# Stick-breaking attention: products of two heads side by side, the causal mask moved onto the exponentials

## The chip, the core and the metric

The kernel runs as one program on one core of a Trainium2 chip. The metric is the device time of one execution in microseconds (us). The engines of the core are TensorE (PE in the rows: matrix products; PEld: its weight loads), VectorE (DVE), ScalarE (ACT), GpSimd (POOL) and SyncE (SP), which issues the transfers. SBUF is the working memory. PSUM is the memory that the products are written to: eight banks of 512 float32 for each of 128 partitions.

## The reference, cut to what matters

The reference is a small network of two blocks on 256 tokens of 1024 features: an attention block with two kinds of heads ("diff" and "moba"), a mixture of 32 experts, a Mamba layer, a gated embedding, a stick-breaking attention and a second gated embedding. The change touches the stick-breaking attention above all, which has 16 heads of 64 features:

```python
for blk in range(s // SB_BLOCK):                      # two blocks of 128 queries
    q0 = blk * SB_BLOCK
    kend = q0 + SB_BLOCK
    z = jnp.einsum('bhtd,bhsd->bhts', q[:, :, q0:kend], k[:, :, :kend])
    strict = s_idx < t_idx
    log_keep = jnp.where(strict, jax.nn.log_sigmoid(-z), 0.0)
    suffix = lax.cumsum(log_keep, axis=3, reverse=True) - log_keep
    weights = jnp.where(strict, jnp.exp(jax.nn.log_sigmoid(z) + suffix), 0.0)
    outs.append(jnp.einsum('bhts,bhsd->bhtd', weights, v[:, :, :kend]))
return (o * jax.nn.silu(gate)) @ w_out
```

Only keys before the query count (`strict`). A head has 128 x 128 scores in its first block of queries and 128 x 256 in its second, 384 columns side by side.

## The kernel before

The program is written with a framework that orders each engine's instructions when it compiles, by the order in which they are emitted and by when it expects their inputs; each engine then works through its own list in order. A tile of a pool is handed on to its next user when all readers of the old one are done, and a pool of `bufs=2` has two such tiles. `mm` puts a product behind the earlier ones into the same PSUM tile.

The eight PSUM banks are: three for the dense products (`dn`), two single ones for the scores (`at`, taken with `ps_at`), two for transposes (`tp`) and one for attention outputs (`pv`).

Dense products split each weight into two parts (`wh` by ScalarE or VectorE, L172 and L176; `wl` by VectorE, L183, or, for some, GpSimd, L187). `nat` yields after each three of its products; `kchunk`, `qchunk` and `vchunk` make the keys, queries and values of eight heads each. `merge` emits two generators side by side, each at the pace of its number of steps. The stick-breaking part is emitted as `stick(0)`, the first eight heads, beside 42 steps (`CUT`) of dense work, and then `stick(1)`, the last eight, beside the other 22; the queries and keys of the last eight heads are made in the first of the two.

`stick_first` makes the weights of one head. Three accumulating products into one bank: a mask of 0 and -1e30 by an identity (`mneg_r`, `ident_r`), then queries times keys for the two blocks of queries, on the lower or upper 64 rows of the array as the head is even or odd. ScalarE takes Abs, Exp and Ln (L1396), which gives ln(1 + exp(-|z|)). VectorE makes max(z, 0) + that (`sp`, L1411) and min(z, 0) - that (`w`, L1413), runs a cumulative sum of `sp` from the right (L1415, restarted at the ends of the blocks by the zeros of `scm`), and subtracts (L1416); ScalarE takes Exp. Two heads later (`LAG`) `stick` transposes the weights (L1432), copies them (L1434) and, for every second head, multiplies two heads with their values (L1442), gates the result and splits it into two parts (L1446 to L1448).

In the first block, `products` (L509) takes two tiles from `ps_at` and issues the score products of two heads in turn, one on the lower and one on the upper half of the array's rows. Its heads run on VectorE in `softmax` (L518).

Of the kernel before, what the change touches and what calls it, by code (L numbers as in the profile page):

```python
# [20 lines left out]
P = 128  # L21
# [7 lines left out]
# columns of the small-parameter pack  # L29
# [9 lines left out]
# columns of the constant packs  # L39
# [25 lines left out]
def merge(*parts):  # L65
    """Runs generators side by side, each at the pace of its number of steps."""
    live = [[g, n, 0] for g, n in parts]
    while live:
        live.sort(key=lambda a: a[2] / a[1])
        a = live[0]  # L70
        a[2] += 1
        try:
            next(a[0])
        except StopIteration:
            live.remove(a)
# [13 lines left out]
class Ring:  # L89
    """Weight tiles of 1 MB in the order of use, loaded ahead into the free slots of a few pools."""  # L90
# [6 lines left out]
    def add(self, name, pool, slots, bufs=None, once=False):  # L97
        """Slots of a tag of a pool, for use again and again or once."""
        self.pools[name] = (pool, bufs or slots, once)
        self.free[name] = self.free.get(name, 0) + slots  # L100
        self.fill()
# [21 lines left out]
    def issue(self):  # L123
        """All reads of the oldest tile taken are in the program."""
# [7 lines left out]
class Halves:  # L132
    """Two tiles [128, 4, 2, 256] as one of [128, 8, 2, 256]."""
# [11 lines left out]
class Dense:  # L145
    """Splits weight tiles into two parts of twelve bits each, ahead of their products."""
# [55 lines left out]
def tile_network(ctx, tc, A, out, dbg=None):  # L202
# [14 lines left out]
    def mm(o, lhsT, rhs, **kw):  # L217
        """A product, issued behind the earlier ones into the same bank."""
# [15 lines left out]

    def ps_at():
        return ps("at", 2, banks[0])
# [14 lines left out]
    # ---------------------------------------------------------------- loads that come first  # L251
# [47 lines left out]
    def keep_warm(n, behind, bank=None):  # L299
        """Products that nobody reads: the tensor engine's clock stays up while it waits for data."""  # L300
# [8 lines left out]
    # ---------------------------------------------------------------- helpers  # L309
    def rsqrt(ss, n, inv):  # L310
        """1 / sqrt(ss * inv + eps) on [128, n]."""
# [6 lines left out]
    def row_scale(tok, junk, behind):  # L318
        """1 / root mean square of each token."""
# [6 lines left out]
    def feed(t, c, outs, src=None):  # L326
        """Half c of the columns of x transposed, times gains: outs are (gain, tile [128, 8, 2, 256] for two parts).

        The products of both token tiles come when the second is there."""
# [31 lines left out]
    def scale_of(t, r, sums, eps=EPS):  # L361
        """1 / root of the sum of the two halves' squares."""
# [8 lines left out]
    def tick():  # L371
        """Half a weight tile has been multiplied: emits what was put off until now."""
# [6 lines left out]
    def nat(dense, xT, groups, evac, bank=ps_dn, by_token=False):  # L379
        """out[token, 512 columns] += xT^T w, weights moving; groups: units (chunk, first block of rows) of a chunk.  # L380

        By token: a unit's two halves for one token tile, then for the other."""
# [28 lines left out]
    def trans(dense, xT, evac):  # L411
        """out[512 columns, token], K = 1024, weights standing; evac gets two blocks of 128 columns."""
# [22 lines left out]
    def head_norm(p, acc, rtok, gain, dst, tok, kb, back=False):  # L435
        """acc [128 tokens, 8 heads x 64] -> root mean square per head, transposed, times the gain.

        acc still lacks the factor rtok of its token."""
# [24 lines left out]
    # ================================================================ first block: attention  # L463
# [45 lines left out]
    def products(q, k, blk, both):  # L509
        """The products of two heads, side by side in the upper and the lower half of the array."""  # L510
        pas = [ps_at() for _ in both]
# [6 lines left out]
    def softmax(pa, b):  # L518
        """Exponentials of the masked scores of one head less their maximum, and 1 / their sums."""
# [16 lines left out]
    def transposed(w):  # L536
        """[128 queries, 384] -> [128 keys, 384]: keys 0.. for all queries, keys 128.. for the later ones."""
# [21 lines left out]
    def forward(b, acc):  # L559
        """The parts of block b of yT, and acc with its queries in their order."""  # L560
# [73 lines left out]
    # bias of a distance, as a Hankel table through DRAM: queries run backwards within their tiles of 128  # L634
    dramp = phA.enter_context(tc.tile_pool(name="dramA", bufs=1, space=DRAM))
    pl = ps_at()
# [13 lines left out]
    # -lambda on all partitions  # L650
# [42 lines left out]
    def turn(t, c):  # L693
        """Half c of the columns of x transposed: after the second token tile."""
# [31 lines left out]
    # ================================================================ router  # L726
# [3 lines left out]
    phP.close()  # L730
    phP = ExitStack()
# [17 lines left out]
    # the first group that has the largest logit  # L749
# [16 lines left out]
    # rank of an expert in its group: the larger logits, and the equal ones before it  # L766
# [14 lines left out]
    # assignments over the 32 experts, and their number up to each token  # L781
# [9 lines left out]
    # place of a token among its expert's slots, from 1 on; 0 where it isn't the expert's  # L791
# [3 lines left out]
    def dispatch(g):  # L795
        """One-hot of the slots of four experts."""
# [6 lines left out]
    # more tokens than slots at any expert?  # L803
# [7 lines left out]
    # weights of the two experts  # L811
# [27 lines left out]
    # ---------------------------------------------------------------- tokens beyond the slots  # L839
# [55 lines left out]
    # ---------------------------------------------------------------- experts, four at a time  # L895
    def combine_T(g):
        """Slot against token for the four experts of g: one-hot, and the weight of each slot."""
# [12 lines left out]
    def gather(g, j, xg):  # L910
        """Transposed inputs of the slots of four experts, four blocks of 128; they lack the factor of their token."""
# [18 lines left out]
    def slot_scale(g):  # L930
        """The factor of each slot's token."""
# [16 lines left out]
    def ple_proj(i):  # L948
        """Half of the embedding's projection."""
# [14 lines left out]
    def in_turn(i):  # L964
        """A product behind the earlier one of the experts: the weights come in this order."""
# [5 lines left out]
    def warm(g, j):  # L971
        """Between the products of the last experts."""
# [3 lines left out]
    def next_xg(g):  # L976
        """The inputs of the four experts after those of g."""
# [75 lines left out]
    phP.close()  # L1053
    phP = ExitStack()
# [3 lines left out]
    # ================================================================ second block: Mamba layer  # L1058
# [29 lines left out]
    def time_steps():  # L1088
        """Time steps, their running sums times A, on [32 heads, 256 tokens]."""
# [4 lines left out]
        pdt = ps_at()  # L1094
# [9 lines left out]
        # ln(1 + e): the logarithm of the rounded sum, and what the rounding took  # L1104
# [26 lines left out]
    # halves: silu(v) = (v/2) (1 + tanh(v/2))  # L1131
# [28 lines left out]
    def gate_z(dst):  # L1160
        """Twice silu."""
# [14 lines left out]
    def ssd(g):  # L1176
        """The state-space heads of group g, gated, with the gain: yTg[g]; rg[g]: 1 / root mean square."""
        pa = ps_at()
# [50 lines left out]
        def sum_up():  # L1229
# [3 lines left out]
            # the squares carry the factor 4 of twice silu  # L1233
# [40 lines left out]
    # ================================================================ gated embedding of a layer  # L1274
    def ple(i, up, sums, then):
        """up holds x times the gain, sums four times the mean squares."""
# [20 lines left out]
        # the last columns one token tile after the other, the end of them in small pieces  # L1297
# [29 lines left out]
    scm = dw_.tile([P, W386], F, name="scm")  # L1327
    nc.sync.dma_start(scm, A["scm"])
    ident_r = dw_.tile([P, P], R, name="ident_r")
    nc.vector.tensor_copy(ident_r, ident)  # L1330
    mneg_r = dw_.tile([P, W386], R, name="mneg_r")
    nc.vector.tensor_copy(mneg_r, mneg)
    sums_k = new_sums()

    def to_stick(tok, c):
# [272 lines left out]
```

## Time and profile before

| what | value |
|---|---|
| time, median of 3 runs | 777.23 us |
| the three runs | 777.46, 773.49, 777.23 us |
| span of the profiled execution, first to last instruction | 773.4 us |
| granted TensorE clock, mean over the span | 0.991 of full speed |
| busy, share of the span: PE, PEld, DVE, ACT, POOL | 95%, 67%, 60%, 49%, 14% |
| stick-breaking part | about 650.5 to 735.5 us of the span |

The profile belongs to one execution, whose span is the time from its first to its last instruction; its own time is not listed apart from the three runs, of which the fastest lies 0.1 us above that span and the median 3.8 us. Busy time is an average over stages with different limits; the stage between 650.5 and 735.5 us is the one to look at here.

### The profile page before, as it was taken

How to read it: one execution, taken by the hardware profiler on the slowest of the kernel's cores; microseconds unless marked ns; L12 is line 12 of the kernel's file. 1: busy time of each engine (PE TensorE's matmuls, PEld its weight loads, DVE VectorE, ACT ScalarE, POOL GpSimd, SP SyncE). 2: the span in 40 equal slices, each digit the busy share in tenths (PEclk: the TensorE clock that was granted, in tenths of full speed). 3: DMA queues.
4: the chain of work that ended last, by engine and by line, in shares of the span. 5: the costliest groups of instructions: out<-in, count | busy, mean ns of one | idle time of the engine just before them, and what ended most of it. 6: DMA issues, size and time to landing. Idle time of an engine off the chain costs nothing. (4 is left out here: it accounts for less than half of the span.)

```text
span 773.4 us, 11374 instructions
## 1 busy us (share of the span) xinstructions
PE 734.3 (95%) x4386; PEld 517.3 (67%) x4386; DVE 467.0 (60%) x887; ACT 380.1 (49%) x712; POOL 110.2 (14%) x74
## 2 busy tenths in 40 slices
PE   8999999997899998899999989999899999999997
PEld 5777767542534334333999988897688897766686
DVE  5658675411101102104999979899888656888974
ACT  6557654210121111103776848475577645756763
POOL 0302300000000000000022231413300301242100
PEclk9999999999899999999999999999999999999999
DMA  8994767899999999983466445444354455222211
GB/s 334 423 404 147 264 238 264 308 412 422 413 422 418 421 420 420 422 369 108 165 242 227 160 151 194 175 164 163 110 184 163 164 177 205 72 104 100 107 56 55
DMA packets 29878, 188.77 MB, mean 244 GB/s; under 512 B 3215, under 2 KB 5852, under 8 KB 8188
## 3 DMA queue, kind: packets, MB, share of 16 engines
q1 hardware_dynamic: 29164, 186.70, 62.5%
q8 instruction: 36, 0.59, 0.3%
q10 hardware_dynamic: 416, 0.62, 0.3%
q0 software_dynamic: 240, 0.67, 0.2%
q14 instruction: 22, 0.18, 0.1%
HBM read 186.88 MB, written 1.10 MB: 243 GB/s over the span
## 5 line engine op out<-in xcount | busy, mean ns | idle before, releaser
L183 DVE TENSOR_TENSOR wl<-w,wh 128x1024 fp32r<-128x1024 f32 x116 | 150.4, 1301 | 49.8 <-ACT wh L172 49.6
L172 ACT ACTIVATE wh<-w 128x1024 fp32r<-128x1024 f32 x117 | 123.1, 1057 | 100.2 <-PE dn L219 86.0
L219 PE MATMUL dn<-uC,wh 128*128 128x256 f32 x640 | 119.5, 288 | 0.6 <-ACT uC L346 0.3
L219 PEld LDWEIGHTS dn<-uC,wh 128*128 128x128 f32 x640 | 100.5, 193 | 2.5 <-issue 1.6
L219 PE MATMUL dn<-uC,wl 128*128 128x256 f32 x320 | 91.2, 285 | 0.0
L187 POOL TENSOR_TENSOR wl<-w,wh 128x1024 fp32r<-128x1024 f32 x18 | 46.6, 2587 | 146.2 <-DVE wh L176 98.4
L997 PE MATMUL pv<-w,xg 128*32 128x512 f32 x512 | 65.8, 596 | 0.0
L219 PEld LDWEIGHTS dn<-uC,wl 128*128 128x128 f32 x320 | 61.9, 193 | 0.2 <-issue 0.2
L315 POOL TENSOR_TENSOR rs_r<-rs_v,mhalf 128x8 f32<-128x8 f32 (+2 forms) x26 | 42.7, 1643 | 119.7 <-DVE rs_v L313 103.5
L928 DVE TENSOR_SCALAR xg<-gx,idg 128x128 f32<-128x128 f32 x30 | 10.5, 350 | 72.0 <-PE gx L219 54.0
L219 PEld LDWEIGHTS gx<-disp,x 128*128 128x128 f32 x240 | 31.1, 200 | 23.6 <-issue 15.3
L219 PE MATMUL dn<-wh,uk 128*128 128x512 f32 x128 | 44.5, 406 | 0.0
L219 PE MATMUL dn<-wh,yTg 128*128 128x512 f32 x128 | 44.2, 407 | 0.3
L219 PE MATMUL gx<-disp,x 128*128 128x128 f32 x240 | 36.2, 296 | 7.7 <-PEq L845 5.0
L936 DVE COPY rs<-tp 128x1 f32<-128x1 f32 x8 | 1.3, 159 | 68.2 <-PE tp L219 68.2
L997 PEld LDWEIGHTS pv<-w,xg 128*32 128x32 f32 x512 | 16.1, 109 | 37.6 <-issue 34.4
L1021 PE MATMUL tp<-w,hT 128*32 128x512 f32 x256 | 37.3, 627 | 1.3 <-DVE hT L1015 1.3
L219 PE MATMUL acc<-oe,cmb 128*128 128x512 f32 x64 | 31.4, 613 | 6.4 <-ACT oe L1027 6.3
L219 PE MATMUL dn<-wh,u 128*128 128x512 f32 x104 | 36.4, 405 | 0.6 <-ACT wh L172 0.6
L926 ACT ACTIVATE xg<-gx,idg 128x128 f32<-128x128 f32 x30 | 11.0, 367 | 52.4 <-DVE xg L928 52.4
L1005 ACT ACTIVATE sl<-pv,rs 128x256 f32<-128x256 f32 x8 | 3.8, 473 | 65.7 <-PE pv L997 37.8
L1027 ACT ACTIVATE oe<-tp,sw 128x512 f32<-128x512 f32 x16 | 11.0, 686 | 43.9 <-PE tp L1021 43.9
(430 smaller groups left out, 1529.0 us busy)
## 6 DMA issues: line engine op xcount, KB each, us to landing
w<-in_wm SPq DMA_DIRECT2D x96, 1024.0 KB, 14.0
w<-in_m SPq DMA_DIRECT2D x28, 1024.0 KB, 4.7
w<-in_ks SPq DMA_DIRECT2D x16, 1024.0 KB, 4.7
w<-in_wi SPq DMA_DIRECT2D x11, 1024.0 KB, 14.3
w<-in_pg SPq DMA_DIRECT2D x8, 1024.0 KB, 4.7
w<-in_wo SPq DMA_DIRECT2D x4, 1024.0 KB, 15.7
eb<-adram SPq DMA_DIRECT2D x8, 512.0 KB, 4.9
w<-in_so SPq DMA_DIRECT2D x4, 1024.0 KB, 4.8
```

The lines of the kernel that those rows point to most:

```text
L172: i = nc.scalar.activation(whf, w, AF.Copy)
L183: i = nc.vector.tensor_tensor(wl.rearrange("p a b -> p (a b)"), w, whf.bitcast(F), op=OP.subtract)
L187: nc.gpsimd.tensor_tensor(wl.rearrange("p a b -> p (a b)"), w, whf.bitcast(F), op=OP.subtract)
L219: i = nc.tensor.matmul(o, lhsT, rhs, **kw)
L315: nc.gpsimd.tensor_tensor(r, v, mhalf.to_broadcast([P, n]), op=OP.pow)
L926: nc.scalar.activation(xg[:, k, :], pg_[:, b * P:(b + 1) * P], AF.Copy, scale=gain_of(5, k))
L928: nc.vector.tensor_scalar(xg[:, k, :], pg_[:, b * P:(b + 1) * P], gain_of(5, k), None, op0=OP.mult)
L936: nc.vector.tensor_copy(rs, pt[:, 0:1])
L997: in_turn(nc.tensor.matmul(pgu[32 * e:32 * e + 32, :], xg[:, k, 32 * e:32 * e + 32], w[:, e * 512:(e + 1) * 512], start=k == 0, stop=k == ...
L1005: nc.scalar.activation(sl, pgu[:, 0:256], AF.Silu, scale=rs)
L1021: in_turn(nc.tensor.matmul(po[32 * e:32 * e + 32, :], hT[:, k, 32 * e:32 * e + 32], w[:, e * 512:(e + 1) * 512], start=k == 0, stop=k == 1 ...
L1027: nc.scalar.activation(oe, po, AF.Copy, scale=sw)
```

## The change

The scores get one tile of two adjacent banks in place of two single banks (`ps_pair`, `bufs=1`); where one bank is wanted, `ps_at` gives out the two halves of such a tile in turn, or a whole pair is taken and half of it used. The first attention's `products` write into such a pair too.

In the stick-breaking part `stick_products` issues the score products of two heads in turn, as `products` does, each pair of heads into one pair of banks. The mask product, its identity and its rounded copy are gone. The scores are now unmasked: `valid` (1 where a key counts) and `anew` (0 where the cumulative sum starts again, at each query's last valid key) are made once, by five small VectorE instructions. Since the sum starts with the key's own term, one subtraction of it from z gives the logarithm of the weight, so the second of the two VectorE instructions on z (L1413) is gone, and z is read by the subtraction instead. After the exponential, GpSimd multiplies the two 128-column triangles of each head by `valid`. The order in `stick` is by pairs: products and weights of a pair, then transposes, copies and value products of the pair before. The value products go through `mm`, too.

```diff
+    halves_at = []
+
+    def ps_pair():
+
+        halves_at.clear()
+        return banks[0].tile([P, 2, 512], F, name="at", tag="at", bufs=1)
+
     def ps_at():
-        return ps("at", 2, banks[0])
+
+        if not halves_at:
+            t = ps_pair()
+            halves_at.extend((t[:, 1, :], t[:, 0, :]))
+        return halves_at.pop()
...
     def products(q, k, blk, both):
-        pas = [ps_at() for _ in both]
+        pair = ps_pair()
+        pas = [pair[:, i, :] for i in both]
...
-    pl = ps_at()
+    pl = ps_pair()[:, 0, :]
...
-        pdt = ps_at()
+        pdt = ps_pair()[:, 0, :]
...
-        pa = ps_at()
+        pa = ps_pair()[:, 0, :]
...
-    scm = dw_.tile([P, W386], F, name="scm")
-    nc.sync.dma_start(scm, A["scm"])
-    ident_r = dw_.tile([P, P], R, name="ident_r")
-    nc.vector.tensor_copy(ident_r, ident)
-    mneg_r = dw_.tile([P, W386], R, name="mneg_r")
-    nc.vector.tensor_copy(mneg_r, mneg)
+    ones_s = dw_.tile([P, W386], F, name="ones_s", tag="pth", bufs=2)
+    nc.sync.dma_start(ones_s, A["scm"])
+
+    valid = dw_.tile([P, W386], F, name="valid")
+    nc.vector.tensor_scalar(valid, mneg, 0.0, None, op0=OP.is_equal)
+    anew = dw_.tile([P, 384], F, name="anew")
+    for to, at, n in ((0, 0, P), (P, 129, SEQ)):
+        nc.vector.tensor_tensor(anew[:, to:to + n], valid[:, at + 1:at + 1 + n], valid[:, at:at + n], op=OP.subtract)
+        nc.vector.tensor_tensor(anew[:, to:to + n], anew[:, to:to + n], ones_s[:, at:at + n], op=OP.add)
...
-    def stick_first(h):
-        rows, blk = slice(64 * (h % 2), 64 * (h % 2) + 64), h // 2
-        pa = ps_at()
-        mm(pa[:, 0:W386], ident_r, mneg_r, start=True, stop=False, skip_group_check=True)
-        mm(pa[:, 0:P], qT2[rows, blk, 0:P], kT[rows, blk, 0:P], start=False, stop=False, skip_group_check=True)
-        mm(pa[:, 129:385], qT2[rows, blk, P:SEQ], kT[rows, blk, :], start=False, stop=True, skip_group_check=True)
-        z = pa[:, 0:W386]
-        e = sd.tile([P, W386], F, name="se", tag="se", bufs=2)
+    def stick_products(b):
+
+        pair = ps_pair()
+        for cols, qs, ks in ((slice(0, P), slice(0, P), slice(0, P)), (slice(P, 384), slice(P, SEQ), slice(0, SEQ))):
+            for i in range(2):
+                rows = slice(64 * i, 64 * i + 64)
+                mm(pair[:, i, cols], qT2[rows, b, qs], kT[rows, b, ks], start=True, stop=True, skip_group_check=True)
+        return pair
+
+    def stick_weights(h, z):
+
+        e = sd.tile([P, 384], F, name="se", tag="se", bufs=2)
         act(e, z, AF.Abs)
         act(e, e, AF.Exp, scale=-1.0)
         act(e, e, AF.Ln, bias=1.0)
...
         nc.vector.scalar_tensor_tensor(sp, z, 0.0, e, op0=OP.max, op1=OP.add)
-        w = sd.tile([P, W386], F, name="swt_", tag="sw", bufs=LAG + 1)
-        nc.vector.scalar_tensor_tensor(w, z, 0.0, e, op0=OP.min, op1=OP.subtract)
-        cum = sd.tile([P, W386], F, name="cum", tag="cum", bufs=2)
-        nc.vector.tensor_tensor_scan(cum[:, ::-1], scm[:, ::-1], sp[:, ::-1], 0.0, op0=OP.mult, op1=OP.add)
-        nc.vector.tensor_tensor(w[:, 0:385], w[:, 0:385], cum[:, 1:386], op=OP.subtract)
-        act(w[:, 0:385], w[:, 0:385], AF.Exp)
+        cum = sd.tile([P, 384], F, name="cum", tag="cum", bufs=2)
+        nc.vector.tensor_tensor_scan(cum[:, ::-1], anew[:, ::-1], sp[:, ::-1], 0.0, op0=OP.mult, op1=OP.add)
+        w = sd.tile([P, 384], F, name="swt_", tag="sw", bufs=4)
+        nc.vector.tensor_tensor(w, z, cum, op=OP.subtract)
+        act(w, w, AF.Exp)
+        for at in (0, SEQ):
+            nc.gpsimd.tensor_tensor(w[:, at:at + P], w[:, at:at + P], valid[:, 0:P], op=OP.mult)
         WS[h] = w
...
-        for h in range(8 * c, 8 * c + 8 + LAG):
-            if h < 8 * c + 8:
-                stick_first(h)
+        for b in range(4 * c, 4 * c + 5):
+            if b < 4 * c + 4:
+                pair = stick_products(b)
+                for i in range(2):
+                    stick_weights(2 * b + i, pair[:, i, 0:384])
+                    yield
+            if b > 4 * c:
+                j = b - 1
+                wts = []
+                for i in range(2):
+                    w = WS.pop(2 * j + i)
+                    pt = ps_tp()
+                    for k in range(3):
+                        nc.tensor.transpose(pt[:, k * P:(k + 1) * P], w[:, k * P:(k + 1) * P], ident)
+                    wts.append(sd.tile([P, 384], F, name="swt", tag="swt", bufs=3))
+                    nc.scalar.activation(wts[-1], pt[:, 0:384], AF.Copy)
+                    yield
+                pv = ps_pv()
+                for part in range(2):
+                    cols, keys = ((slice(0, SEQ), slice(0, SEQ)), (slice(P, SEQ), slice(SEQ, 384)))[part]
+                    for i in range(2):
+                        mm(pv[64 * i:64 * i + 64, cols], v[:, part, (2 * j + i) * 64:(2 * j + i + 1) * 64],
+                           wts[i][:, keys], start=part == 0, stop=part == 1, skip_group_check=True)
...
```

## Rows read from the trace of the kernel before

**Rows 1.** Windows: busy us of each engine (instructions), granted clock, DMA share, GB/s
```profile
650.50:700.90 50.40, 48.45 (x240) 34.68 (x239) 41.02 (x62) 33.27 (x61) 16.67 (x8) 1.00 0.31 111
700.90:735.50 34.60, 34.60 (x170) 22.80 (x169) 31.64 (x50) 24.12 (x49) 5.17 (x2) 1.00 0.26 91
```

**Rows 2.** Chain that ended last: start, us, work
```profile
708.83 1.03 PE at L219 x5
```

**Rows 3.** Timeline of PE, one head of the stick-breaking part: start, us
```profile
653.10 0.40 PE L219 MATMUL dn<-wh,uk 128*128 128x512 f32 x1
653.33 0.34 PE L219 MATMUL at<-mneg_r,ident_r 128*128 128x386 f32 x1
653.60 0.92 PE L219 MATMUL at<-kT,qT 64*128 64x128 f32 x4
...
654.78 0.40 PE L219 MATMUL dn<-wl,uk 128*128 128x512 f32 x1
```

**Rows 4.** Timeline of PE, one pair of heads of the first attention
```profile
47.41 0.39 PE L219 MATMUL dn<-wh,u 128*128 128x512 f32 x1
47.73 0.93 PE L219 MATMUL at<-qk 64*128 64x128 f32 x8
48.58 0.51 PE L219 MATMUL dn<-wh,u 128*128 128x512 f32 x1
48.93 0.40 PE L219 MATMUL dn<-wl,u 128*128 128x512 f32 x1
```

**Rows 5.** Timeline of PE, first and last of a later pair's four pieces
```profile
111.64 0.49 PE L219 MATMUL at<-km,qm 64*128 64x128 f32 x2
...
114.52 0.70 PE L219 MATMUL at<-km,qm 64*128 64x256 f32 x2
```

**Rows 6.** Timeline of ACT and DVE, the first head
```profile
651.95 0.50 ACT L1396 ACTIVATE se<-at 128x386 f32<-128x386 f32 x1
...
652.48 1.09 ACT L1396 ACTIVATE se<-se 128x386 f32<-128x386 f32 x2
...
653.60 0.56 DVE L1411 SCALAR_TENSOR_TENSOR sp<-at,se 128x386 f32<-128x386 f32 x1 [0.47 <-ACT se L1396]
...
654.08 0.55 DVE L1413 SCALAR_TENSOR_TENSOR swt__6144<-at,se 128x386 f32<-128x386 f32 x1
...
654.54 0.95 DVE L1415 TENSOR_TENSOR_SCAN cum<-scm,sp 128x386 f32<-128x386 f32 x1
...
655.53 0.56 DVE L1416 TENSOR_TENSOR swt__6144<-swt__6144,cum 128x385 f32<-128x385 f32 x1
```

**Rows 7.** Two-input instructions on SBUF, three lines: ns min/median/max
```profile
L1224 POOL TENSOR_TENSOR sqs<-sqs,ysq x12: 727/1150/1528, 442.3 to 556.1; 128x256 f32<-128x256 f32 x12
...
L187 POOL TENSOR_TENSOR wl<-w,wh x18: 2395/2513/3389, 389.0 to 722.3; 128x1024 fp32r<-128x1024 f32 x18
L183 DVE TENSOR_TENSOR wl<-w,wh x116: 1187/1220/3085, 8.5 to 760.8; 128x1024 fp32r<-128x1024 f32 x116
```

**Rows 8.** Timeline of POOL and DVE around 710 us
```profile
709.14 2.57 POOL L187 TENSOR_TENSOR wl<-w,wh 128x1024 fp32r<-128x1024 f32 x1 [8.39 <-DVE wh L176]
...
710.01 0.55 DVE L1413 SCALAR_TENSOR_TENSOR swt__6635<-at,se 128x386 f32<-128x386 f32 x1
...
710.48 2.05 DVE L1415 TENSOR_TENSOR_SCAN cum<-scm,sp 128x386 f32<-128x386 f32 x1
```

**Rows 9.** Groups of DVE, 650.5 to 736 us: busy us, mean ns | idle before
```profile
L183 DVE TENSOR_TENSOR wl<-w,wh 128x1024 fp32r<-128x1024 f32 x12 | 18.9, 1578 | 4.2 <-ACT wh L172 4.2
L1415 DVE TENSOR_TENSOR_SCAN cum<-scm,sp 128x386 f32<-128x386 f32 x16 | 16.9, 1058 | 0.0
```

**Rows 10.** Timeline of the last eight heads: first and last products, last gating
```profile
701.24 0.92 PE L219 MATMUL at<-kT,qT 64*128 64x128 f32 x4
...
724.57 0.92 PE L219 MATMUL at<-kT,qT 64*128 64x128 f32 x4
...
735.52 0.42 DVE L1446 TENSOR_TENSOR so<-pv,sgT 128x256 f32<-128x256 f32 x1 [0.60 <-PE pv L1442]
```

More of the change, by code (lines that the diff above doesn't have):

```diff
@@ L730, in tile_network @@
     phP.close()
+    halves_at.clear()
     phP = ExitStack()
@@ L1053, in tile_network @@
     phP.close()
+    halves_at.clear()
     phP = ExitStack()
@@ L1409, in stick_first @@
         act(e, e, AF.Ln, bias=1.0)
-        sp = sd.tile([P, W386], F, name="sp", tag="sp", bufs=2)
+        sp = sd.tile([P, 384], F, name="sp", tag="sp", bufs=2)
         nc.vector.scalar_tensor_tensor(sp, z, 0.0, e, op0=OP.max, op1=OP.add)
-        w = sd.tile([P, W386], F, name="swt_", tag="sw", bufs=LAG + 1)
-        nc.vector.scalar_tensor_tensor(w, z, 0.0, e, op0=OP.min, op1=OP.subtract)
-        cum = sd.tile([P, W386], F, name="cum", tag="cum", bufs=2)
-        nc.vector.tensor_tensor_scan(cum[:, ::-1], scm[:, ::-1], sp[:, ::-1], 0.0, op0=OP.mult, op1=OP.add)
@@ L1418, in stick_first @@
         WS[h] = w
     def stick(c):
-        wts = []
-        for h in range(8 * c, 8 * c + 8 + LAG):
-            if h < 8 * c + 8:
-                stick_first(h)
-                yield
-            if h >= 8 * c + LAG:
-                j = h - LAG
-                w = WS.pop(j)
-                pt = ps_tp()
-                for b, at in enumerate((0, 129, 129 + P)):
-                    nc.tensor.transpose(pt[:, b * P:(b + 1) * P], w[:, at:at + P], ident)
-                wts.append(sd.tile([P, 384], F, name="swt", tag="swt", bufs=3))
-                nc.scalar.activation(wts[-1], pt[:, 0:384], AF.Copy)
-                yield
-                if j % 2:
-                    b = j // 2
-                    pv = ps_pv()
-                    for part in range(2):
-                        cols, keys = ((slice(0, SEQ), slice(0, SEQ)), (slice(P, SEQ), slice(SEQ, 384)))[part]
-                        for i in range(2):
-                            nc.tensor.matmul(pv[64 * i:64 * i + 64, cols], v[:, part, (j - 1 + i) * 64:(j + i) * 64],
-                                             wts[i][:, keys], start=part == 0, stop=part == 1, skip_group_check=True)
-                    wts = []
-                    o = sd.tile([P, SEQ], F, name="so", tag="so", bufs=2)
-                    nc.vector.tensor_tensor(o, pv[:, 0:SEQ], sgT[:, b, :], op=OP.mult)
-                    nc.scalar.activation(oT[:, b, 0, :], o, AF.Copy)
-                    nc.vector.tensor_tensor(oT[:, b, 1, :], o, oT[:, b, 0, :].bitcast(F), op=OP.subtract)
-                    yield
@@ new lines, in stick @@
+        for b in range(4 * c, 4 * c + 5):
[21 more added lines that the diff above has]
+                           wts[i][:, keys], start=part == 0, stop=part == 1, skip_group_check=True)
+                o = sd.tile([P, SEQ], F, name="so", tag="so", bufs=2)
+                nc.vector.tensor_tensor(o, pv[:, 0:SEQ], sgT[:, j, :], op=OP.mult)
+                nc.scalar.activation(oT[:, j, 0, :], o, AF.Copy)
+                nc.vector.tensor_tensor(oT[:, j, 1, :], o, oT[:, j, 0, :].bitcast(F), op=OP.subtract)
+                yield
```

## The prediction

> **What bounds the kernel now.** I read the windows of the stick-breaking part first. From 650.5 to 735.5 us TensorE is busy for 48.5 of 50.4 us and 34.6 of 34.6 us, with its clock at full speed, 2.4 GHz [rows 1]. VectorE has 9.4 us to spare in the first half and 3.0 us in the second, where it is 91% busy [rows 1]. The chain that ended last runs through TensorE's products in the second half, head after head; one head's score products take 1.03 us of it [rows 2]. So two engines matter: TensorE sets the end, and VectorE is close behind it in the second half. Work taken from TensorE alone moves the end only until VectorE, or the string of dependent steps of a pair of heads, takes over.
>
> **TensorE: what goes.** In the timeline of one head, the mask starts at 653.33 us, the products at 653.60, and the second dense product after them at 654.78. Dense products start 0.23 us apart (653.10, 653.33), so the head costs 654.78 - 653.33 - 0.23 = 1.22 us with its changes of shape, 2.44 us for two heads [rows 3]. The changed order is already in the first attention: a pair's eight products, of the same shapes, take 0.93 us, where four of one head take 0.92 us [rows 3, 4]. The two halves of the array therefore work at the same time. From the dense product at 47.41 us to the one at 48.93, less two of 0.23 us, a pair costs 1.06 us [rows 4]. The saving is 2.44 - 1.06 = 1.38 us a pair, 11.0 us for eight pairs, 5.5 us in each half.
>
> **VectorE: what goes.** One of four instructions of a head: `w` starts at 654.08 and the next at 654.54, so 0.46 us, 7.4 us for 16 heads, 3.7 us a half [rows 6]. The subtraction reads z from PSUM now; I take its 0.56 us as it is, since instructions that read z take 0.55 us [rows 6].
>
> **GpSimd: what comes.** Thirty-two products of 128 x 128, which the trace does not show. The nearest rows are its two-input instructions: 0.73 us at the fastest for 256 columns and 2.40 us for 1024, so 2.17 ns a column and 0.45 us for 128; the upper bound is the median of the 256-column form, 1.15 us [rows 7]. That is 14 to 37 us of GpSimd, which is busy for 21.8 us of 85 [rows 1], so the engine itself has room. Each head's transposes come 0.9 us later at the lower price. Beside other heads' work that costs nothing; behind the last head nothing is left to cover it, and I count 1.0 us.
>
> What GpSimd takes from VectorE is the larger matter. At 709.14 us GpSimd splits a weight for 2.57 us; the scan that VectorE starts at 710.48 takes 2.05 us in place of 0.95 and ends after GpSimd has, while the instruction at 710.01, which reads PSUM, keeps its 0.55 us [rows 6, 8]. In the whole part, twelve splits on VectorE took 18.9 us where the median would give 12 x 1.22 = 14.6, and 16 scans 16.9 us where 0.95 would give 15.2: 6.0 us lost beside GpSimd's five weight splits of 2.51 us, 0.48 us for each us of GpSimd [rows 7, 9]. For masks of 0.45 us that is 0.22 us each, 6.9 us in all, 3.5 us a half. So VectorE keeps nearly what it has: 31.6 - 3.7 + 3.5 = 31.4 us in the second half. The Trainium skill says of this ("SBUF — State Buffer", Who interferes with whom) that a VectorE instruction with two SBUF inputs contends with a GpSimd instruction that reads SBUF, and that the one that issues second fully blocks; the scan agrees (2.05 us against 0.95) and so does the undisturbed PSUM reader. By that rule alone a mask could cost VectorE its whole 0.45 us, 14.4 us in all: that is a rival below.
>
> **The single pair of banks: what is added as a wait.** Before, a bank was free again after `w`, and each head had its own. Now the next pair's products wait until both heads' subtractions are done. Behind the waiting products on TensorE stand dense products, which the compiled order may or may not have put ahead of them; ScalarE's Abs waits for the products. The string of one pair: products 0.92 us; Abs, Exp and Ln of two heads, 2 x 1.62 us (651.95 to 653.57); then sum, scan and subtraction of the second head, 0.48 + 0.99 + 0.56 = 2.03 us [rows 4, 6]. With the handoffs that is 6.3 us at the least; VectorE's load gives 31.4 / 4 = 7.9 us a pair, and I take that. In the first half four pairs at 7.9 us (32 us) lie well inside 50.4 - 5.5 = 44.9 us, so TensorE stays the bound and the 5.5 us are gained. In the second half the first and the last head's products were 724.57 - 701.24 = 23.3 us apart, and 10.95 us went by from the last to its gating at 735.52 [rows 10]. After, three steps of 7.9 us make 23.7 us, and the tail is 10.95 + 1.0 us: 1.4 us longer than before. The 5.5 us that TensorE saves there are given back as its idle time.
>
> **The rest.** First attention: a later pair is cut into four pieces, first 0.49 and last 0.70 us, two of each kind, 2.4 us in place of 0.93, because its two banks came free one after the other [rows 4, 5]. Five of the eight pairs are cut, the others into fewer pieces; one pair of banks keeps the eight products free to stand together. That is worth nothing (if the wait for the second bank costs what it saves) to some 5 us; waiting is the price of it, so I take 1.2 us. The five setup instructions replace two casts; at the 0.46 us of a 386-column instruction [rows 6] they are 2.3 us at most, early in a stage where VectorE waits for ScalarE's splits; taken as nothing, at worst 1 us. The other users of the scores' banks take one at a time, far apart: nothing.
>
> **Sum.** First half -5.5, second half +1.4, first attention -1.2: -5.3 us, from a span of 773.4 us to 768.1. The three runs before lie 0.1 to 4.1 us above that span, their median 3.8; the same distance puts the changed median at 771.9. I round to 771.5.
>
> **Rivals.**
> - TensorE stays the bound everywhere: the pair's string packs to 6.3 us and VectorE fills its waits with weight splits. For it: the 3.0 us idle and the lighter VectorE instruction list. Against it: 91% busy now. Then -11.0 - 1.2 to -5 us: 761 to 765.
> - The gain is lost: in-order lists let other work (a split of 1.22 us, a copy) in between the steps of a pair, and its string takes 9 us. Then the second half is 3 x 9 + 12 = 39 us, 4.7 us longer, and with the first half's 5.5 the total is -2: about 775. The same comes out if the products do not do what the change says: if dense products fall between a pair's pieces as in the first attention [rows 5], mostly the mask's 16 x 0.27 us [rows 3] is saved, and less after the masks.
> - Slower: each mask blocks VectorE's scan or split for its whole length. VectorE then has 72.7 - 7.4 + 14.4 = 79.7 us of work; with the 12.3 us of waits that it has now [rows 1] the part takes 92 us, 7 us longer: about 784. It decides from 0.35 us lost per mask (65.3 + 12.3 + 32 x 0.35 = 88.8, 3.8 us above 85.0); the trace's rate gives 0.22.
>
> **How the numbers follow.** Half a per cent (3.9 us) is about what a measurement of this kernel tells from no change; the three runs scatter by as much. Forecast (-4 to -9 us) 0.42, TensorE bound throughout 0.16, gain lost 0.25, slower 0.17. So faster 0.58, same 0.25, slower 0.17. The likeliest case by itself is 768 to 774. The range takes in most of the two neighbours and the beginning of the slower case: 763 to 780.
>
> **What would show it.** Eight products of about 0.93 us in one piece for each pair, and no mask product. The stick-breaking part some 4 us shorter, with TensorE idle for several us in its second half, most of it before score products or transposes. VectorE without L1413's kind; scans that still reach 1.2 to 1.5 us beside masks. Steps from one pair's products to the next near 7.9 us in the second half. Wrong would make it: steps under 7 us with TensorE still full (a larger gain); masks of 1 us and more, or VectorE waiting at GpSimd's roots of head norms, which stand in one list with the masks (a loss); or a shift in the first attention beyond 3 us.

## The result, and the profile after

The changed kernel takes 817.6 us (median of four runs, 815.7 to 817.8) where the kernel before, timed beside it, takes 775.4: a ratio of 1.053, interval 1.050 to 1.057. I had forecast 771.5 and a range that ended at 780. The profiled execution has a span of 816.1 us for 773.4, and a mean granted clock of 0.962 for 0.991.

Windows of the changed kernel: from the first score product to that of the fifth pair, on to the last pair, and to the end; then two stretches of the second half. They answer to [rows 1].

```profile
654.90:716.80 61.90, 52.11 (x239) 35.79 (x238) 39.52 (x54) 32.81 (x60) 24.74 (x22) 0.94 0.29 105
716.80:762.20 45.40, 33.38 (x133) 20.48 (x133) 23.30 (x34) 20.43 (x40) 9.60 (x13) 0.76 0.20 70
762.20:816.10 53.90, 42.74 (x197) 33.31 (x197) 25.70 (x41) 23.43 (x43) 3.67 (x8) 0.82 0.06 20
...
735.00:750.00 15.00, 9.83 (x38) 5.84 (x38) 4.98 (x9) 6.38 (x14) 2.64 (x6) 0.69 0.21 71
750.00:762.00 12.00, 7.60 (x20) 4.16 (x20) 5.92 (x9) 4.41 (x9) 1.49 (x2) 0.50 0.00 1
```

The same from the first score product to the end in the kernel before:

```profile
651.00:773.40 122.40, 116.02 (x581) 85.37 (x580) 94.69 (x145) 75.29 (x140) 22.75 (x11) 1.00 0.25 87
```

The stretch takes 161.2 us for 122.4. So 38.8 of the 42.7 us lie here: 11.7 up to the fifth pair (61.9 for 50.2), 22.0 from there to the last pair (45.4 for 23.4) and 5.1 behind it (53.9 for 48.8). The other 3.9 were lost ahead of the stretch. TensorE, which was the bound, is idle for 33.0 us (161.2 - 128.2) where it was idle for 6.4. VectorE is no fuller (88.5 us for 94.7). No engine is the bound: something waits. TensorE's busy time rose too, by 12.2 us, though it has less to do: its granted clock fell to 0.76 of full speed in the second half and to 0.50 from 750 to 762 us, which is the lower level, 1.2 GHz.

The timeline of the first pair after, ScalarE, VectorE and TensorE, answers to [rows 3, 6]:

```profile
654.90 0.93 PE L219 MATMUL at<-kT,qT 64*128 64x128 f32 x8
...
655.88 0.49 ACT L1413 ACTIVATE se<-at 128x384 f32<-128x384 f32 x1
...
659.10 0.56 DVE L1436 TENSOR_TENSOR swt__6140<-at,cum 128x384 f32<-128x384 f32 x1
...
659.69 0.53 ACT L1413 ACTIVATE swt__6140<-swt__6140 128x384 f32<-128x384 f32 x1 [2.21 <-DVE swt__6140 L1436]
660.12 0.47 ACT L1413 ACTIVATE se<-at 128x384 f32<-128x384 f32 x1
...
666.12 0.55 DVE L1436 TENSOR_TENSOR swt__6159<-at,cum 128x384 f32<-128x384 f32 x1
...
666.81 0.93 PE L219 MATMUL at<-kT,qT 64*128 64x128 f32 x8
```

The eight products of a pair stand together here and take 0.93 us. But the second head's first step, the Abs at 660.12, whose input was there at 655.8, stands in ScalarE's list behind the first head's last exponential, which waits 2.21 us for VectorE's subtraction. The two heads run one after the other, and only then do the next pair's products start: 11.9 us from pair to pair here. In the second half the step is 15.1 us ((762.18 - 716.80) / 3), where I had put 7.9.

The later pairs' products, same timeline, TensorE:

```profile
716.80 0.49 PE L219 MATMUL at<-kT,qT 64*128 64x128 f32 x4 [0.23 <-DVE swt__6431 L1436]
...
721.52 0.70 PE L219 MATMUL at<-kT,qT 64*128 64x256 f32 x4
...
734.15 0.93 PE L219 MATMUL at<-kT,qT 64*128 64x128 f32 x8 [1.34 <-DVE swt__6604 L1436]
...
747.10 1.33 PE L219 MATMUL at<-kT,qT 64*128 64x128 f32 x8 [2.02 <-DVE swt__6642 L1436]
...
762.18 1.65 PE L219 MATMUL at<-kT,qT 64*128 64x128 f32 x8 [1.55 <-DVE swt__6722 L1436]
```

The fifth pair is cut in two; the other seven stand together. The last three wait for the second head's subtraction, with TensorE idle for 1.3 to 2.0 us. The same eight products take 1.33 us while the granted clock falls (0.87 from 746 to 748 us) and 1.65 us at the lower level (0.50 from 762 to 764 us). The masks show as a wait as well: a head's transposes stand behind them.

```profile
758.04 0.90 PE L1457 MATMUL tp<-idg,swt__6706 128*128 128x128 f32 x3 [1.49 <-POOL swt__6706 L1439]
```

### The profile page after: what moved, and what is told of

Same layout as the page of the kernel before. It is cut to its first block, busy times and chain, and to the rows that moved or that the text cites. A ratio compares the mean times of both kernels' runs of the same rounds, so it can differ in the third digit from the quotient of the medians.

```text
span 816.1 us, 11366 instructions
## 1 busy us (share of the span) xinstructions
PE 745.4 (91%) x4370; PEld 519.4 (64%) x4370; DVE 462.4 (57%) x874; ACT 381.5 (47%) x712; POOL 123.9 (15%) x106
## 5 line engine op out<-in xcount | busy, mean ns | idle before, releaser
L183 DVE TENSOR_TENSOR wl<-w,wh 128x1024 fp32r<-128x1024 f32 x116 | 148.0, 1281 | 49.8 <-ACT wh L172 49.4
L326 POOL TENSOR_TENSOR rs_r<-rs_v,mhalf 128x8 f32<-128x8 f32 (+2 forms) x26 | 39.6, 1527 | 112.3 <-DVE rs_v L324 72.7
L1034 PE MATMUL tp<-w,hT 128*32 128x512 f32 x256 | 34.5, 602 | 1.3 <-DVE hT L1028 1.3
L219 PE MATMUL dn<-wh,oT 128*128 128x512 f32 x64 | 28.0, 498 | 3.9 <-ACT oT L1469 3.9
```

The costliest lines, as they stand in the source:

```text
L183: i = nc.vector.tensor_tensor(wl.rearrange("p a b -> p (a b)"), w, whf.bitcast(F), op=OP.subtract)
L219: i = nc.tensor.matmul(o, lhsT, rhs, **kw)
L326: nc.gpsimd.tensor_tensor(r, v, mhalf.to_broadcast([P, n]), op=OP.pow)
L1034: in_turn(nc.tensor.matmul(po[32 * e:32 * e + 32, :], hT[:, k, 32 * e:32 * e + 32], w[:, e * 512:(e + 1) * 512], start=k == 0, stop=k == 1 ...
```

## The experiments

**Theory A**: with one tile of two banks, the framework keeps the readers of a pair in the order in which they are written, across engines and though they read different banks, so the heads run one after the other. **Theory B**: GpSimd's masks hold up the transposes. **Theory C**: a pair's two banks are handed on together, and that costs what the products save. The stage from the router's logits to the Mamba layer's first root, ahead of the stick-breaking part, moves from one execution to the next: two of the kernels below, whose programs are the same up to there, took 230.2 and 226.6 us for it. So beside each time stands the stretch from the first score product to the end, from the one profiled execution of each kernel (before 122.4, after 161.2).

**Two tiles.** The changed kernel with each head of a pair in a tile of its own bank, and single banks where one is wanted; no other edit.

```diff
-    halves_at = []
+    class Two:
+        def __init__(self):
+            self.t = [ps("at", 2, banks[0]) for _ in range(2)]
+
+        def __getitem__(self, key):
+            return self.t[key[1]][key[0], key[2]]
 
     def ps_pair():
-
-        halves_at.clear()
-        return banks[0].tile([P, 2, 512], F, name="at", tag="at", bufs=1)
+        return Two()
...
```

> The changed kernel with the scores in two tiles of one bank each, as before, in place of one tile of two banks, everywhere; all else of the change stays. Theory A (the one tile of two banks makes the second head's Abs on ScalarE stand behind the first head's subtraction on VectorE, so that the two heads of a pair run one after the other): the second Abs follows the first within a microsecond, a pair goes from some 14 us back to 7 to 9 us, TensorE's clock stays up, and the time falls from 817 to 765 to 785 us. Theory B (GpSimd's multiplications and the waits for them make the loss): at least 800 us, with the transposes still waiting for GpSimd. Theory C (only that a pair's banks are handed on together): between, some 785 to 800 us. The first attention should give back what it lost in any case, so that the first score product of the stick-breaking part comes at about 651 us in place of 655.

Measured: 782.8 us, ratio to before 1.008 (1.005 to 1.011); the stretch 129.2 us. The stretch has the same instructions (566 of TensorE, 129 of VectorE, 141 of ScalarE, 43 of GpSimd in both); only what is one tile has changed, and with it the compiled order, and 32.0 us of the stretch come back. In ScalarE's list the two Abs of a pair now start within 1.0 us of each other, in seven of eight pairs back to back, as in the first:

```profile
655.36 0.87 ACT L1410 ACTIVATE se<-at 128x384 f32<-128x384 f32 x2
```

One thing expected did not come: the first score product is at 654.40 us, not at about 651. The first attention did give back what it lost (scores at 47.67 us, logits at 135.9), but the stage behind it took 230.2 us in this execution, for 228.0 in the kernel before.

**Both Abs first.** One tile as in the changed kernel, but both Abs of a pair written ahead of the first head's other steps.

```diff
...
                 pair = stick_products(b)
+                es = [stick_abs(pair[:, i, 0:384]) for i in range(2)]
                 for i in range(2):
-                    stick_weights(2 * b + i, pair[:, i, 0:384])
+                    stick_weights(2 * b + i, pair[:, i, 0:384], es[i])
```

> The changed kernel with the one tile of two banks kept, and one thing moved: Abs of both heads of a pair is emitted ahead of the rest of either. Theory A: nothing is left that holds the second head back, a pair takes 8 to 9 us, the time falls to 770 to 790 us; some 4 us stay lost ahead of the stick-breaking part. Theory B: 805 us or more. Theory C (the handing on of two banks at once is the loss): hardly changed, 805 us or more, too.

Measured: 793.4 us, ratio 1.021 (1.017 to 1.025), stretch 137.1: 24.1 us back, a little less than expected (770 to 790). The order in which two lines are written is worth that much, with both banks still handed on together; 7.9 us remain between this and two tiles.

**No masks.** The changed kernel leaves GpSimd's multiplications out.

```diff
-        for at in (0, SEQ):
-            nc.gpsimd.tensor_tensor(w[:, at:at + P], w[:, at:at + P], valid[:, 0:P], op=OP.mult)
```

> The changed kernel without GpSimd's multiplications by the mask, so that the weights of keys that do not count stay in the sums. Theory A: the heads still run one after the other; each pair saves at most the 0.9 us of its last head's two multiplications, and the time is 800 to 813 us. Theory B: the loss goes, below 785 us.

Measured: 807.3 us, ratio 1.038 (1.034 to 1.043), stretch 150.4. The masks cost 10.8 us; they are not the main cause.

**The first attention alone.** The kernel before, with the one tile everywhere but in the stick-breaking part.

> The kernel before, with the one tile of two banks in the first attention alone. If that is where the 4 us ahead of the stick-breaking part come from: 777 to 781 us, the first score product of the stick-breaking part at 653 to 656 us in place of 650.7. If they come from elsewhere (the order of the later stages): no change within 0.5%.

Measured: 779.6 us, ratio 1.004 (1.002 to 1.006), stretch 122.3, as before: all of it ahead of the stick-breaking part. Its timeline shows a wait that I had ruled out:

```profile
21.38 0.81 PE L219 MATMUL at<-oh,sm 33*12 33x384 f32 x2
23.59 0.50 PE L219 MATMUL at<-wh,u 128*128 128x512 f32 x1 [1.40 <-ACT lrow L651]
```

and its window from 20 to 30 us what followed:

```profile
20.00:30.00 10.00, 8.60 (x30) 6.09 (x29) 6.04 (x9) 3.74 (x5) 4.87 (x3) 0.83 1.01 423
```

The bias table's small product takes the pair's tile for itself, and the next projection, which had the second bank before, waits 1.40 us for ScalarE's copy. In this execution the granted clock is 0.83 over the ten us (0.50 from 25 to 28); in the changed kernel's own, with the same wait, it is 1.00. The first attention's scores start at 50.87 us here and at 49.97 there, for 47.73 before [rows 4].

**Masks in the scan.** Two tiles, and the mask made without an instruction of its own: a running sum of thousands at the masked columns, which the existing factor 0 clears at the first valid one.

```diff
+    nc.vector.memset(anew[:, P - 1:P], 1e4)
...
-        nc.vector.tensor_tensor_scan(cum[:, ::-1], anew[:, ::-1], sp[:, ::-1], 0.0, op0=OP.mult, op1=OP.add)
+        nc.vector.tensor_tensor_scan(cum[:, ::-1], anew[:, ::-1], sp[:, ::-1], 1e4, op0=OP.mult, op1=OP.add)
...
-        for at in (0, SEQ):
-            nc.gpsimd.tensor_tensor(w[:, at:at + P], w[:, at:at + P], valid[:, 0:P], op=OP.mult)
```

> The two-tile kernel without any mask on GpSimd and without a mask product: the scan starts from 1e4 instead of 0 at its first (masked) column, and its factor at column 127 is 1e4, so that every masked column has a running sum of thousands and its exponential comes out as zero. Nothing is left out, and VectorE's instructions per head stay three. Theory A plus masks (what is left of the loss once the second head's Abs no longer waits is the transposes and head norms that stand behind masks in GpSimd's list): about 10 us less than the 782.8 us of two tiles, 770 to 775. Rival (what is left is the handing on of both banks at once, so that a pair's products wait for two subtractions): 780 or more, TensorE's waits before the products on the subtraction stay (0.7 to 1.6 us each).

Measured: 773.8 us, ratio 0.997 (0.995 to 1.000), stretch 120.0, 9.2 less than with GpSimd's masks. So B holds for some 9 to 11 us (9.2 here, 10.8 above). The timeline of the two-tile kernel shows how they cost it, GpSimd and TensorE:

```profile
694.12 3.22 POOL L325 TENSOR_TENSOR rs_r<-rs_v,mhalf 128x8 f32<-128x8 f32 x2
...
696.68 1.08 PE L467 MATMUL tp<-idg,sq 128*128 128x128 f32 x4 [2.88 <-DVE sq L456]
...
713.15 3.32 POOL L187 TENSOR_TENSOR wl<-w,wh 128x1024 fp32r<-128x1024 f32 x1
716.44 0.86 POOL L1436 TENSOR_TENSOR swt__6619<-swt__6619,valid 128x128 f32<-128x128 f32 x2
...
716.94 0.90 PE L1454 MATMUL tp<-idg,swt__6619 128*128 128x128 f32 x3 [2.90 <-POOL swt__6619 L1436]
```

Two masks take 0.86 us, but they queue behind a weight split of 3.32 us, and the roots of the head norms behind masks and splits; TensorE waits 2.9 us each time. (Of the wait at the head norm 1.94 us remain without masks, as shown further below.) The waits before products that theory C needs did not go (0.74, 0.73 and 2.19 us remain in the kernel with scan masks), and yet it is as fast as before.

**The arithmetic alone.** The kernel before with no mask product, the new three VectorE steps and the scan's mask, one head after the other as before.

> The kernel before with its own order, one head after the other and each head in its own bank, but with the changed arithmetic: no mask product on TensorE, one VectorE subtraction less, the mask made in the scan. Products of two heads are not brought together. If the arithmetic by itself is sound and only the pairs are to blame: TensorE saves 16 x 0.27 = 4.3 us and VectorE 16 x 0.46 = 7.4 us, so 769 to 772 where before is at 776. If VectorE reading z from PSUM for longer (the subtraction holds the bank until after the scan, some 2 us more per head) costs what that saves: 775 to 780.

Measured: 776.6 us, ratio 1.001 (0.999 to 1.003), stretch 122.0. No gain, as in the second case expected. TensorE has 4.1 us less of score products and masks there (14.7 for 18.8); one wait of products for the subtraction shows, 1.09 us at 710.90, and why the rest is not gained no run settles.

**The pairs alone.** The kernel before with its mask products and four VectorE steps, the products of two heads chained.

```diff
...
+        for part, (cols, qs, ks) in enumerate(((slice(0, P), slice(0, P), slice(0, P)),
+                                               (slice(129, 385), slice(P, SEQ), slice(0, SEQ)))):
+            for i in range(2):
+                rows = slice(64 * i, 64 * i + 64)
+                m = mm(pas[i][:, cols], qT2[rows, b, qs], kT[rows, b, ks], start=False, stop=part == 1,
+                       skip_group_check=True)
+                after(m, last)
+                last = m
...
```

> The kernel before with one part of the change alone: the four products of each of two heads are issued as one chain of eight, after both mask products, in two single banks; mask product, VectorE's four instructions and the order of everything else are those of before. If bringing the products together is free: TensorE saves 2 x 0.92 - 0.93 = 0.91 us a pair, 7.3 us in all, of which the TensorE-bound first half keeps its share: 769 to 773. If waiting for two banks at once costs what it saves: 775 to 781, with TensorE idle before the mask products until the second head's VectorE reads are done.

Measured: 779.3 us, ratio 1.003 (1.001 to 1.005), stretch 125.3. Pairs without the lighter arithmetic lose a little. That is the size that C expects, but not its mechanism: the idle time is not in front of the products but at the weighted values and a head norm in the first half, 3.04 us for VectorE's read of the one bank they share:

```profile
700.05 0.65 PE L1459 MATMUL pv<-swt,v 128*64 128x256 f32 x2 [3.04 <-DVE so L1463]
```

**Both together**, in the order of before and with two single banks:

> The one-head-at-a-time arithmetic of the second kernel of this call and the chained eight products of the third together: what the change was meant to be, with two single banks, no masks on GpSimd, and the heads' transposes spread out as before. If pairs, masks and the one tile were the whole trouble: TensorE saves 11 us of products, the first half keeps 5.5 and the second what VectorE's lighter list allows: 763 to 768, faster than every kernel so far. If the handing on of two banks at once is the trouble: 775 or more.

Measured: 773.4 us, ratio 0.997 (0.995 to 0.999), stretch 120.2. That lies between the two cases expected. Neither part gained by itself; together they are faster than before, by 0.3%.

**One tile, both Abs first, masks in the scan**, to see whether the costs add:

> The changed kernel with its pair of banks as one tile everywhere, both Abs emitted ahead of the first head's other steps, and the masks made in the scan (start value 1e4, factor 1e4 at column 127; nothing is left out) in place of GpSimd's. If the order of reads in the one tile and the masks are two costs that add, it stands to the kernel with both Abs first (793.4) as the two-tile kernel with scan masks stands to the one with GpSimd masks (9 us from the first score products to the end): 784, and the 8 us that one tile costs more than two tiles even so stay. If those 8 us were only masks that met a pair handed on at once, it comes within 2 us of the two-tile kernel with scan masks plus the 3 us of the first attention: 775 to 779.

Measured: 783.2 us, ratio 1.011 (1.008 to 1.014), stretch 128.2. They add, as the first case has it (784): 8.9 us less than with GpSimd's masks, 8.2 more than two tiles. Its timeline of VectorE shows what the tile still orders:

```profile
656.02 0.56 DVE L1437 SCALAR_TENSOR_TENSOR sp<-at,se 128x384 f32<-128x384 f32 x1 [0.80 <-ACT se L1414]
656.61 0.96 DVE L1439 TENSOR_TENSOR_SCAN cum<-anew,sp 128x384 f32<-128x384 f32 x1
657.60 0.56 DVE L1441 TENSOR_TENSOR swt__6143<-at,cum 128x384 f32<-128x384 f32 x1
658.08 0.55 DVE L1437 SCALAR_TENSOR_TENSOR sp<-at,se 128x384 f32<-128x384 f32 x1
658.66 0.96 DVE L1439 TENSOR_TENSOR_SCAN cum<-anew,sp 128x384 f32<-128x384 f32 x1
...
660.65 0.55 DVE L1441 TENSOR_TENSOR swt__6158<-at,cum 128x384 f32<-128x384 f32 x1
```

and the same of two tiles with masks in the scan:

```profile
652.31 1.02 DVE L1430 SCALAR_TENSOR_TENSOR sp<-at,se 128x384 f32<-128x384 f32 x2 [0.78 <-ACT se L1411]
653.25 1.80 DVE L1432 TENSOR_TENSOR_SCAN cum<-anew,sp 128x384 f32<-128x384 f32 x2
654.97 0.53 DVE L1434 TENSOR_TENSOR swt__6152<-at,cum 128x384 f32<-128x384 f32 x1
655.42 0.55 DVE L1434 TENSOR_TENSOR swt__6169<-at,cum 128x384 f32<-128x384 f32 x1
```

With one tile the second head's sum comes behind the first head's subtraction, and another split gets in between; with two tiles both heads go side by side and the subtractions are 0.45 us apart, not 3.05. This is one pair; how much of the 8 us is this order, and how much the handing on of both banks at once, no run separates.

**The bias product elsewhere**, and the best of all with the first attention's pair. The edit, against the kernel of the first attention alone:

```diff
-    pl = ps_pair()[:, 0, :]
+    pl = ps_pv()
```

> The kernel before with the one tile of two banks in the first attention alone, as in the earlier run at 779.6 us, with one more edit: the small product of the bias table goes into the bank of the weighted values, which nobody uses by then, and not into the pair. There the trace of that run shows TensorE waiting 1.40 us for ScalarE's copy of that product at 23.59 us, and 0.83 of the clock granted from 20 to 30 us. If this one wait and the clock after it are the whole 3 us: the wait is gone, the first score products come at 47.7 to 47.9 us as in the kernel before (50.87 with the wait), and the time is 775 to 776.5, level with before or a little under. If the pairs of the first attention themselves cost the 3 us: 779 to 780 again.

> The kernel with chained pairs in two single banks and the masks in the scan (773.4 us), with the first attention's pairs in one tile and the bias product out of it. If the first attention's pairs are worth what its stretch showed (from the first score products to the router's logits 87.3 us for 88.3): 772 to 773, the fastest of all. If that stretch is paced by its weights: 773 to 774.

Measured: 777.2 us, ratio 1.003 (1.001 to 1.004), and 773.1 us, ratio 0.998 (0.996 to 0.999). The first is 0.7 us above what its better case expected, the second at the border of its two cases. In both the wait is gone and the first scores come at 47.95 and 47.96 us. From there to the router's logits both take 86.3 us (88.3 before). But the first kernel's profiled execution, at 780.1 us the longest of its twelve, then had the clock at 0.63 from 136 to 142 us, the second, with the same program up to there, at 1.00; from the logits to the Mamba layer's first root the one took 233.4 us, the other 228.5, the kernel before 228.0. What the earlier time is worth behind a stage paced by its weights (DMA share 0.93 to 0.95) these runs don't settle, nor why the first of them stays 0.3% slow.

## Why the prediction was wrong

The loss of 38.8 us in the stretch, by the runs: Abs behind the first head's exponential 24.1 (161.2 - 137.1), the rest of what one tile costs 7.9 (137.1 - 129.2), masks on GpSimd 9.2 (129.2 - 120.0), and a gain of 2.4 from what was meant (122.4 - 120.0). Each is a difference of two profiled executions; the medians of the times step down alike, by 24.2, 10.6 (with some 3 of the first attention) and 9.0. What the lower clock cost is within these sums; no run separated it.

- **The step that failed: the string of one pair, 7.9 us.** I wrote that ScalarE's Abs waits for the products, and then laid the three steps of two heads end to end on ScalarE beside the first head's VectorE work. That overlap was assumed; with one tile it is not there, and the step measured 15.1 us. With both Abs first it is 12.5 us ((745.51 - 708.05) / 3), with two tiles 9.9 ((734.74 - 705.12) / 3), and with the scan's mask as well 7.9 ((722.59 - 698.86) / 3):

```profile
698.86 0.93 PE L219 MATMUL at<-kT,qT 64*128 64x128 f32 x8
...
722.59 1.35 PE L219 MATMUL at<-kT,qT 64*128 64x128 f32 x8
```

  So of the 7.2 us too much, 5.2 are the one tile and 2.0 the masks. That 7.9 itself came out is in part luck: I took it from a VectorE that is busy throughout, and VectorE is busy for 19.4 of those 23.7 us, 6.5 a pair. Of the rivals, "the string takes 9 us" came nearest, with far too small a price (at 15.1 its formula gives 3 x 15.1 + 12 = 57 us for 34.6 in the second half) and mostly another cause: it has splits and copies between the steps, where the one tile holds the second head behind the first.
- **TensorE's saving** was about right: score products and masks 18.8 us busy before, 9.3 in the kernel with chained pairs and scan masks and 9.5 in that with two tiles and scan masks, so some 9.4 less where I had 11.0 with the changes of shape; a pair takes 0.93 us.
- **"TensorE stays the bound in the first half and the 5.5 us are gained"** failed on its own, also with the tile repaired. From the first to the fifth pair it took 50.2 us before and 49.7 with two tiles and scan masks. The window of that kernel:

```profile
649.20:698.90 49.70, 45.69 (x233) 33.54 (x232) 37.63 (x55) 31.27 (x61) 14.75 (x7) 0.97 0.32 110
```

  and its timeline of TensorE and GpSimd there:

```profile
655.65 1.35 PE L219 MATMUL at<-kT,qT 64*128 64x128 f32 x8 [0.74 <-DVE swt__6152 L1434]
...
674.11 0.86 PE L219 MATMUL pv<-swt,v 128*64 128x256 f32 x6 [0.68 <-ACT swt L1455]
...
685.22 2.38 POOL L187 TENSOR_TENSOR wl<-w,wh 128x1024 fp32r<-128x1024 f32 x1 [6.86 <-issue]
687.56 3.23 POOL L325 TENSOR_TENSOR rs_r<-rs_v,mhalf 128x8 f32<-128x8 f32 x2
...
690.12 1.06 PE L467 MATMUL tp<-idg,sq 128*128 128x128 f32 x4 [1.94 <-DVE sq L456]
```

  TensorE is idle for 4.0 us there, where it was for 1.9 before, and after the longest wait its clock is granted at 0.54 and 0.61 (690 to 692 and 692 to 694 us; 0.97 over the window). Work taken from TensorE lets it arrive sooner at results that come no sooner: the head norm's roots stand behind a weight split in GpSimd's list. (In the kernel before, the chain of the second half was TensorE alone [rows 2].)
- **The second half's +1.4.** With two tiles and GpSimd's masks, the kernel that the sum describes, it is 29.6 us from the fifth to the last pair, not 23.7, and the tail behind the last products is 48.9 us, as before (48.8) and not 1.0 longer. Without GpSimd's masks it is 23.7 and 46.6.
- **Masks.** 0.45 us was right for a mask alone (two in 0.86 us); on average they took 0.57 us in the changed kernel, 0.66 with two tiles and 0.75 with both Abs first. That later transposes "cost nothing beside other heads' work" was wrong: 9 to 11 us.
- **The port.** My 0.22 us of VectorE per mask was wrong, and so was the slower rival. The groups of scans, first of two tiles with GpSimd's masks, then of two tiles without:

```profile
L1431 DVE TENSOR_TENSOR_SCAN cum<-anew,sp 128x384 f32<-128x384 f32 x16 | 16.1, 1040 | 0.1
```

```profile
L1432 DVE TENSOR_TENSOR_SCAN cum<-anew,sp 128x384 f32<-128x384 f32 x16 | 16.1, 1037 | 0.1
```

  In the other two pairs of kernels that differ in the masks alone the scans average 1308 ns with them and 1261 without (both Abs first), and 1030 with and 1181 without (the changed kernel); the weight splits 1306 and 1385, 1328 and 1304, 1321 and 1318. So VectorE did not lose what I had put down; the masks were stretched instead. The Trainium skill ("SBUF — State Buffer", Who interferes with whom) has the one that issues second blocked; here that is mostly the short mask, which takes up to 1.0 us with two tiles and 1.3 with both Abs first. I had carried the loss beside a weight split of 2.5 us over to masks of 0.45.
- **"The other users take one at a time, far apart: nothing"** failed: the bias product's wait is 1.40 us, and the first scores came 2.2 us late, 0.6 of it from ahead of this wait. The first attention's own pairs were about as forecast: 87.3 us from scores to logits for 88.3 (-1.0 for -1.2, a value that I had picked from 0 to 5), with three of the eight pairs still cut. Of the 3.9 us lost ahead of the stretch 1.3 are there at the logits; 2.5 come in the stage behind (230.5 for 228.0), within what it moves by between executions.

## What to carry to other kernels

Give heads that should overlap a tile each: a tile that spans two banks may put everything that reads it into one order, and the price (32 us here) shows as a step in the engines' lists, not as a busier engine. (The runs show what the tile and the order of the lines are worth; by which rule the framework orders the readers they do not show.) Before costing a string of steps over two engines, read from the lists which instruction stands behind which, because an engine that works through its list in order and waits for the first head does nothing for the second. And where an engine will then wait for results that others make, expect little of a saving on it: 9 us less of score products and masks came out as 2 to 3 us of time.

## What the chip showed that I had not expected

Idle time at TensorE was paid for twice here. From 733 us on TensorE waits 1.34, 0.45, 0.58 and 0.97 us between products, and the granted clock is 0.50 from 738 to 744 us. It is 0.98 from 744 to 746, and after the wait of 2.02 us before 747.10 it is 0.50 again, from 748 to 770 us with further waits; score products take 1.65 us there for 0.93. One pause does not settle it: the wait of 1.40 us at 23.59 us is followed by 0.50 from 25 to 28 us in one kernel, while the changed kernel, with the same wait at 24.27, shows 1.00 in its window from 20 to 30 us:

```profile
20.00:30.00 10.00, 8.60 (x38) 6.18 (x37) 6.63 (x10) 4.20 (x6) 4.87 (x3) 1.00 1.02 426
```
